# Graph attention on one core: warm-up matmuls, counts between merge steps, one layout for the bins, and a last block of 96 destinations

## The chip, the cores and the metric

The kernel runs on one core of a Trainium2 chip. The metric is the device time of one execution in microseconds (us), the median of several executions. A core has five engines with a queue each: TensorE (PE, matmuls, with its weight loads listed apart as PEld), VectorE (DVE), ScalarE (ACT), GpSimd (POOL) and SyncE (SP), which here only issues transfers. Engines wait for each other through semaphores.

## The reference, cut to what matters

```
num_nodes, in_features, out_features, num_edges, n_heads = 4096, 64, 64, 50000, 4
x_proj[h] = x @ weight[h]
score[h, i] = leaky( x_proj[h, src_i] . att_src[h] + x_proj[h, dst_i] . att_dst[h] )     # slope 0.2
output[h, dst_i] += exp(score[h, i]) * x_proj[h, src_i]                                  # all edges i
output[h, d] /= sum of exp(score[h, i]) over the edges i with dst_i = d, plus 1e-8
return output as [4096, 4 * 64]
```

Edges come as two lists of 50,000 node numbers, in no order. The work is a gather by source, a weight per edge and head, and a sum by destination.

## The kernel before, in words

**Keys.** Each of 128 partitions takes 391 edges. An edge becomes one number, `key`, which orders edges by group of source (16 groups of 256 nodes), then destination, then source within the group. VectorE computes it in two halves, L695 to L698, from the tiles `eS` and `eD`, which are loaded in two parts.

**First sort.** VectorE sorts the keys by compare-exchange steps on 128x512 tiles: `flip` (L190, L192) and `half` (L201, a pair of operations: minimum and maximum). `rows` sorts each partition, and `runs` then merges runs of eight partitions with the help of 32x32 transposes (`turn`, L230). Beside it ScalarE counts with 16 sign activations (`below`, L269) how many keys of each partition lie below each group bound, TensorE adds the counts of a run in two small matmuls (`counts`, L280), and it prepares the tables (`tables`, L404 to L425): `xa` with x and each source's part of the score, `adb` with each destination's part and an identity matrix. `store` (L261, SP) writes the sorted runs to DRAM. `bounds` (L289 to L295) turns the counts into the start and end of each stretch, `ws1` and `we1`. `fetch` converts the start to integer (`wi`, L352) and gathers `raw` from DRAM with two indirect transfers (L354, POOL): each partition gets the part of one run that belongs to its group.

**Second sort.** `group` merges again with VectorE, by destination now. ScalarE's 33 sign activations count against the bounds of 33 blocks of 125 destinations (BD), TensorE adds them, and VectorE turns them into offsets (`Stretches`, L310 to L320) between the last half steps. On these half steps also hang `relative` and `split` (L720 to L724), which prepare block 0 straight from the sorted keys. `turn` (80 matmuls, L372) and `warm` (5 matmuls, L377) use TensorE without anyone reading the result. The sorted keys `ki` are stored (L261), and five windows `win` are gathered from them (L354, POOL), one for every eight blocks.

**Bins.** `Windows.unpack(i)` (L442 to L447) splits a window into destination within the block and source, as bf16 tiles `tb`; VectorE does it for window 0, VectorE and POOL for the others. SP stores them in `gat_bins` in DRAM (L449). `load(b)` (L472, SP) reads a block's bins back, the same 8 KB into every partition (`bc`, four buffers). For blocks 0 and 1 `spread` does without DRAM: TensorE copies rows across partitions (L483) and ScalarE or VectorE writes them to `bc` (L485).

**The loop over 33 blocks.** `onehot(b)`: VectorE compares `bc` with the partition number, L498 for destinations and the lower 128 sources of a group, L501 for the upper 128. `gather(b, c)` in three chunks of 6, 6 and 4 tiles: TensorE multiplies the one-hots with `xa` and `adb` (L519, L521, L525), which gathers features and scores and forms the one-hot of destinations per edge; ScalarE writes exp of the scores (`ex`, L527) and the gathered rows (`xs`, L529). `weights` (L539) and `values` (L547): VectorE forms the edge weights `wv` and weighted features `val`. `sums`: TensorE adds them by destination into `acc` (L563 for the weights, L570 for the features). `take` (L624, L626): ScalarE copies `acc` to `aT`. `project` (L631), `invert` (L636), `give` (L644, with the store L646) multiply by `weight`, divide and write the output. The last block holds 4096 - 32 x 125 = 96 destinations; its features are summed into two tiles of their own, and its output is written in two halves.

All engine queues follow the order in which the code issues instructions, since the whole part runs under a manual schedule; nothing is reordered by a planner. The part under `tc.If` handles inputs whose stretches overflow a window, and doesn't run here.

Of the kernel before, what the change touches and what calls it, by code (L numbers as in the profile page):

```python
# [11 lines left out]
P = 128  # L12
# [26 lines left out]
def kernel(ctx: ExitStack, tc: tile.TileContext, x: bass.AP, edge_index: bass.AP,  # L39
# [22 lines left out]
    bin_dram = nc.dram_tensor("gat_bins", (8 * NI, 2, NR, W2), BF16).ap()  # L62
# [100 lines left out]
    Wbd = cst.tile([P, 2, P], F32)  # L163
    ws1 = cst.tile([P, 2], F32)
# [7 lines left out]
    class Sorter:  # L172
# [59 lines left out]
        def runs(self, to=None, fine=0, between=()):  # L232
# [12 lines left out]
            for m in range(1, 3):  # L245
                self.turn()
                self.opposed(m)
                for j in range(m - 1, -1, -1):
                    self.half(j)
                self.turn()  # L250
                last = fine if m == 2 else 0
                todo = list(between) if m == 2 else []
                for j in range(8, last - 1, -1):
                    self.half(j, to=to if m == 2 and j == last else None)
                    if todo:
                        todo.pop(0)(self.a[self.cur])
                assert not todo
# [26 lines left out]
    def bounds(pool, cps, nt, n, off, mask, nk, ws, we):  # L284

        ni = ws.shape[1] // len(cps)
        for i, ps in enumerate(cps):
            cnt = pool.tile([P, nt + 1], F32, name=f"cnt{i}")
            V.tensor_scalar(out=cnt[:], in0=ps[:], scalar1=-0.5, scalar2=RUN * n / 2, op0=OP.mult, op1=OP.add)  # L289
            for o, t in ((0, ws), (1, we)):  # L290
                pick = pool.tile([P, ni, nk], F32, name=f"pick{i}{o}")
                V.tensor_tensor(out=pick[:], in0=av(cnt[:], o, [nk, ni], [1, nk]),
                                in1=av(mask[:], 0, [0, ni], [1, nk]), op=OP.mult)
                V.tensor_reduce(out=t[:, i * ni:(i + 1) * ni], in_=pick[:], axis=AX, op=OP.add)
                V.tensor_tensor(out=t[:, i * ni:(i + 1) * ni], in0=t[:, i * ni:(i + 1) * ni],  # L295
                                in1=av(off[:], i, [0, ni]), op=OP.add)
# [60 lines left out]
    PAGE = 80  # L357

    def group(pool, pp, start, between=()):
# [8 lines left out]
        if between:  # L368

            turn = pp.tile([P, L], F32, name="turn")  # L370
            for i in range(PAGE):
                T.matmul(out=turn[:, 0:32], lhsT=identb[:], rhs=identb[:, 0:32], start=True, stop=True)  # L372
        st = Stretches(pool, counts(pool, pp, sgn, 8 * NI, [sel2[:]])[0])
        if between:
            warm = pp.tile([P, L], F32, name="warm")
            for i in range(5):
                T.matmul(out=warm[:], lhsT=identb[:], rhs=adb[:, 0:4, 0:P], start=True, stop=True)  # L377
# [53 lines left out]
    class Windows:  # L431
# [8 lines left out]
        def unpack(self, i, *engs):  # L440
# [7 lines left out]
            for k, eng in enumerate(engs):  # L448
                eng.dma_start(out=dataclasses.replace(bin_dram[8 * i, k], ap=[[2 * NR * W2, 8], [W2, NR], [1, W2]]),  # L449
                              in_=self.tb[:, i, k, :])  # L450
# [6 lines left out]
    class Blocks:  # L457
# [11 lines left out]
        def load(self, b):  # L469
            if b < ND:  # L470
                t = self.bcp.tile([P, 2, NT * W2], BF16, name="bc")
                nc.sync.dma_start(out=t[:], in_=dataclasses.replace(bin_dram[b], ap=[[0, P], [NT * W2, 2],  # L472
                                                                                    [1, NT * W2]]))
                self.bc[b] = t

        def spread(self, b, c, tb, row, copy):

            if c == 0:
                self.bc[b] = self.bcp.tile([P, 2, NT * W2], BF16, name="bc")
            t0, n = CH[c]  # L480
            ps = self.psx.tile([P, CH[0][1], PW], F32, name="ps")
            for i in range(n):
                T.matmul(out=ps[:, i, :], lhsT=av(identb[:], row(t0 + i), [0, P]), rhs=tb, start=(i % 2 == 0),  # L483
                         stop=True, skip_group_check=True)
            copy(out=av(self.bc[b][:], t0 * W2, [W2, n], [NT * W2, 2], [1, W2]),  # L485
                 in_=av(ps[:], 0, [PW, n], [W2, 2], [1, W2]))

        def onehot(self, b, t0=0, nt=NT, halves=(0, 1)):
            if b >= ND:
                return  # L490
            if t0 == 0 and halves[0] == 0:

                self.oh[b] = self.bp.tile([P, 3, NT * W2], BF16, name="oh")
            oh, bc = self.oh[b], self.bc[b]
            e = slice(t0 * W2, (t0 + nt) * W2)
            for i in halves:
                if i == 0:
                    V.tensor_scalar(out=oh[:, 0:2, e], in0=bc[:, :, e], scalar1=pF[:, 0:1], scalar2=None,  # L498
                                    op0=OP.is_equal)
                else:  # L500
                    V.tensor_scalar(out=oh[:, 2, e], in0=bc[:, 1, e], scalar1=pF[:, 1:2], scalar2=None,  # L501
                                    op0=OP.is_equal)

        def gather(self, b, c):
# [10 lines left out]
            ps = self.psx.tile([P, CH[0][1], PW], F32, name="ps")  # L515
            for i in range(n):
                t = t0 + i
                e = slice(t * W2, (t + 1) * W2)
                T.matmul(out=ps[:, i, P:P + XC], lhsT=oh[:, 1, e], rhs=xa[:, 2 * t, :], start=(i % 2 == 0), stop=False,  # L519
                         skip_group_check=True)  # L520
                T.matmul(out=ps[:, i, 0:S0], lhsT=oh[:, 0, e], rhs=adb[:, b, :], start=False, stop=False,  # L521
                         skip_group_check=True)
            for i in range(n):
                t = t0 + i
                T.matmul(out=ps[:, i, P:P + XC], lhsT=oh[:, 2, t * W2:(t + 1) * W2], rhs=xa[:, 2 * t + 1, :],  # L525
                         start=False, stop=True, skip_group_check=True)
# [25 lines left out]
        def sums(self, b, k):  # L552
# [3 lines left out]
            if k < 0:  # L556
                self.acc = self.psa.tile([P, AW], F32, name="acc")
                self.to = [self.acc[:, i * BD:(i + 1) * BD] for i in range(2)]
                if apart:
                    self.to = [self.psx.tile([P, CH[0][1], PW], F32, name="ps")[:, 0, 0:BD] for i in range(2)]  # L560
# [8 lines left out]
            for t in range(NT):  # L569
                T.matmul(out=self.to[k], lhsT=val[:, t, k * P:(k + 1) * P], rhs=xs[:, t, 0:BD],  # L570
# [38 lines left out]
    class Finish:  # L609
# [8 lines left out]
        def take(self, b, acc, at=0):  # L618
            n = acc.shape[-1]
            if n != BD:  # L620
# [4 lines left out]
            if n != BD:  # L625
                S.activation(out=self.aT[b][:, 2 * BD:AW], in_=acc[:, n - H:n], func=ACTF.Identity, bias=eps[:, 0:1])  # L626

        def project(self, b):
            self.pf = self.psf.tile([P, C], F32, name="pf")
            for k in range(2):  # L630
                T.matmul(out=self.pf[:, k * P:(k + 1) * P], lhsT=self.aT[b][:, k * BD:k * BD + P], rhs=Wbd[:, k, :],  # L631
# [6 lines left out]
        def give(self, b, parts=1):  # L638
# [3 lines left out]
            for k, eng in zip(range(parts), (nc.sync, nc.scalar)):  # L642
                h = slice(k * nh, (k + 1) * nh)
                V.tensor_tensor(out=res[0:BD, h], in0=av(self.pf[0:BD], k * nh * Dout, [Dout, nh], [1, Dout]),  # L644
                                in1=av(self.inv[0:BD], k * nh, [1, nh], [0, Dout]), op=OP.mult)
# [34 lines left out]
    with tc.tile_pool(name="sort1", bufs=1) as so1, tc.tile_pool(name="pre", bufs=1) as pr, \  # L680
# [3 lines left out]
        tF = so1.tile([P, EL], F32)  # L684
# [6 lines left out]
        for e, n in ((0, EH), (EH, EL - EH)):  # L691
# [3 lines left out]
            V.tensor_scalar(out=sli[:, c], in0=src, scalar1=SG - 1, scalar2=None, op0=OP.bitwise_and)  # L695
            V.tensor_scalar(out=tF[:, c], in0=sli[:, c], scalar1=1.0 - N, scalar2=None, op0=OP.mult)
            V.scalar_tensor_tensor(out=uF[:, c], in0=dst, scalar=float(SG), in1=tF[:, c], op0=OP.mult, op1=OP.add)
            V.scalar_tensor_tensor(out=key[:, c], in0=src, scalar=float(N), in1=uF[:, c], op0=OP.mult, op1=OP.add)  # L698
        tables(pr, pps, pp1)
        so.rows(1, EL)  # L700
        cps = counts(so1, pp1, sgn, NR, [sel1[:, 0, :], sel1[:, 1, :]])
        store(skey1, so.runs())
        bounds(so1, cps, NR, EL, off1, m16, NR, ws1, we1)
    with ExitStack() as st:
# [3 lines left out]
        class Lent:  # L708


            def tile(self, shape, dt, name):
                return blocks.sink.psf.tile(shape, dt, name=name, tag="pf")

# [15 lines left out]
        stretches = group(so2, Lent(), ws1[:], (relative, split))  # L729
# [8 lines left out]
        win.unpack(0, nc.sync, nc.sync)  # L738
# [15 lines left out]
        for i in range(1, NI):  # L754
            win.unpack(i, nc.sync, nc.sync)
        blocks.sums(0, 1)
        blocks.onehot(2)
# [65 lines left out]
```

## Time and profile before

| | |
|---|---|
| median of 5 executions | 292.8 us (292.29 to 293.94) |
| the profiled execution's own time | 290.6 us |
| its span, first to last instruction | 288.5 us |
| mean granted TensorE clock | 0.851 |
| busy: VectorE, TensorE, ScalarE, GpSimd | 261.4, 205.7, 190.8, 33.3 us |
| first sort stored (issue) | 68.20 us |
| second sort stored (issue) | 113.46 us |
| first whole one-hot of the loop, block 2 | 129.18 us |
| one block of the loop | 4.7 us |
| last output issued | 282.3 us |

In a row of the timeline the first number is the start in us from the span's start, the second the time until the group's last instruction ends, then engine, line, operation and operands as output<-input, and in brackets the idle time ahead of it with what ended it. `x2` means two instructions of a kind in a row. `SPq` is the issue of a transfer by SP, not the transfer itself. In the row PEclk each digit is TensorE's granted clock in tenths, in 40 equal slices of the span.

### The profile page before, as it was taken

To read this page: it belongs to the slowest core of one execution; us is meant where nothing else is said; L and a number is where in the kernel's file an instruction comes from. 1 tells how busy PE (TensorE), PEld (TensorE's weight loads), DVE (VectorE), ACT (ScalarE), POOL (GpSimd) and SP (SyncE) were. 2 spreads that over 40 slices of the span, in tenths; PEclk is the share of its full clock that TensorE was granted. 3 is DMA by queue.
4 is the path that set the end of the run, shared out by engine and by line. 5 is a ranking of instruction groups with operands and counts; after the bars stand their busy time and mean duration, and the time that the engine had idled before them with its cause. 6 is when DMAs were issued, how large, how long until landed. Compare 5 with 4: busy or idle time off the path is not lost.

```text
span 288.5 us, 8664 instructions
## 1 busy us (share of the span) xinstructions
PE 205.7 (71%) x3593; PEld 197.3 (68%) x3593; DVE 261.4 (91%) x528; ACT 190.8 (66%) x392; POOL 33.3 (12%) x81
## 2 busy tenths in 40 slices
PE   0000899992000008698999999999999999999980
PEld 0000599992000004498999999999999999999980
DVE  5999999997399999979999999999999999999960
ACT  2960620013399965757888888888888888888850
POOL 7882000000200000752000000000000000000000
PEclk9999975555555555869999999999999999999997
DMA  3007000001100001187868686868676777765011
GB/s 111 0 21 145 0 2 0 0 1 40 36 0 0 0 0 37 45 265 275 332 251 276 224 287 220 290 207 297 225 284 222 279 233 260 250 250 182 26 38 38
DMA packets 13328, 40.77 MB, mean 141 GB/s; under 512 B 3120, under 2 KB 8912, under 8 KB 9312
## 3 DMA queue, kind: packets, MB, share of 16 engines
q1 hardware_dynamic: 10768, 37.91, 37.5%
q10 hardware_dynamic: 1808, 1.56, 2.3%
q0 software_dynamic: 704, 0.66, 1.2%
q8 instruction: 30, 0.49, 0.7%
q14 instruction: 18, 0.15, 0.2%
HBM read 35.08 MB, written 5.05 MB: 139 GB/s over the span
## 4 chain that ended last, share of the span: by engine, by line


## 5 line engine op out<-in xcount | busy, mean ns | idle before, releaser
L529 ACT CAST xs<-ps 128x1200 bf16<-128x1200 f32 (+1 forms) x99 | 103.9, 1050 | 0.0
L547 DVE TENSOR_TENSOR val<-xs,wv 128x4096 bf16<-128x4096 bf16 (+1 forms) x34 | 75.4, 2219 | 0.4 <-ACT xs L529 0.2
L570 PE MATMUL acc<-xs,val 128*128 128x125 bf16 x1024 | 62.6, 220 | 0.0
L521 PE MATMUL ps<-adb,oh 128*128 128x136 bf16 x528 | 62.2, 225 | 0.0
L519 PE MATMUL ps<-xa,oh 128*128 128x72 bf16 x528 | 59.6, 197 | 2.1 <-ACT aT L624 1.1
L570 PEld LDWEIGHTS <-val 128*128 128x128 bf16 x1056 | 59.6, 99 | 0.2
L521 PEld LDWEIGHTS <-oh 128*128 128x128 bf16 x528 | 49.6, 99 | 1.3 <-issue 1.2
L519 PEld LDWEIGHTS <-oh 128*128 128x128 bf16 x528 | 47.4, 99 | 1.4 <-DVE oh L498 1.4
L498 DVE TENSOR_SCALAR oh<-bc,pF 128x4096 bf16<-128x4096 bf16 (+2 forms) x37 | 42.5, 1148 | 1.1 <-ACT bc L485 0.7
L527 ACT ACTIVATE ex<-ps 128x96 bf16<-128x96 f32 (+1 forms) x99 | 25.0, 252 | 23.2 <-PE ps L525 23.1
L201 DVE TENSOR_TENSOR sA<-sB 128x256 f32<-128x256 f32 (+2 forms) x104 | 37.2, 399 | 1.7
L201 DVE TENSOR_TENSOR sB<-sA 128x256 f32<-128x256 f32 (+2 forms) x98 | 35.1, 399 | 1.6
L525 PE MATMUL ps<-xa,oh 128*128 128x72 bf16 x528 | 33.5, 198 | 0.0
L280 PE MATMUL cnt_ps<-sgn,sel 128*128 128x17 f32 (+1 forms) x6 | 1.7, 390 | 39.1 <-ACT sgn L272 39.1
L280 PEld LDWEIGHTS cnt_ps<-sgn,sel 128*128 128x128 f32 x6 | 1.4, 317 | 39.2 <-issue 39.1
L525 PEld LDWEIGHTS <-oh 128*128 128x128 bf16 x528 | 26.5, 99 | 0.1
L421 PEld LDWEIGHTS at_ps<-uv,xT 64*128 64x128 f32 x130 | 26.3, 313 | 0.2 <-issue 0.2
L421 PE MATMUL at_ps<-uv,xT 64*128 64x4 f32 x130 | 26.4, 339 | 0.0
L501 DVE TENSOR_SCALAR oh<-bc,pF 128x2048 bf16<-128x2048 bf16 (+2 forms) x37 | 25.6, 692 | 0.0
L269 ACT ACTIVATE junk<-kr,nb 128x512 f32<-128x512 f32 x33 | 23.8, 722 | 1.1
L631 PE MATMUL pf<-Wbd,aT 128*128 128x128 f32 x132 | 22.6, 294 | 0.8 <-ACT aT L624 0.8
L404 PE MATMUL ps<-ident,wS 64*128 64x64 f32 x2 | 0.7, 352 | 28.2 <-DMA wS<-in_weight_dram 28.2
(144 smaller groups left out, 248.3 us busy)
## 6 DMA issues: line engine op xcount, KB each, us to landing
bc<-gat_bins SPq DMA_DIRECT2D x31, 1024.0 KB
out_dram<-res SPq DMA_DIRECT2D x32, 125.0 KB
eD<-in_edge_index_dram ACTq DMA_DIRECT2D x2, 195.0 KB
eS<-in_edge_index_dram SPq DMA_DIRECT2D x2, 195.0 KB
gat_bins<-tb SPq DMA_DIRECT2D x10, 32.0 KB
gat_sorted<-sA SPq DMA_DIRECT2D x1, 256.0 KB
gat_sorted<-ki SPq DMA_DIRECT2D x1, 256.0 KB
win<-gat_sorted,to POOLq DMA_INDIRECT x5, 2.6
```

What stands on the lines that cost most here:

```text
L201: V.tensor_tensor(out=av(d[:], o, [2 * h, n], [1, h]), in0=av(s[:], 0, [2 * h, n], [1, h]), in1=av(s[:], h, [2 * h, n], [1, h]), op=op)
L269: S.activation(out=junk[:], in_=v, func=ACTF.Sign, bias=nbnd[:, b:b + 1], scale=1.0, accum_out=sgn[:, b:b + 1])
L421: T.matmul(out=ps[:, b, :], lhsT=xT[:, b * step:b * step + P], rhs=uv[:, k, :], start=(b == 0), stop=True, skip_group_check=True)
L498: V.tensor_scalar(out=oh[:, 0:2, e], in0=bc[:, :, e], scalar1=pF[:, 0:1], scalar2=None, op0=OP.is_equal)
L501: V.tensor_scalar(out=oh[:, 2, e], in0=bc[:, 1, e], scalar1=pF[:, 1:2], scalar2=None, op0=OP.is_equal)
L519: T.matmul(out=ps[:, i, P:P + XC], lhsT=oh[:, 1, e], rhs=xa[:, 2 * t, :], start=(i % 2 == 0), stop=False, skip_group_check=True)
L521: T.matmul(out=ps[:, i, 0:S0], lhsT=oh[:, 0, e], rhs=adb[:, b, :], start=False, stop=False, skip_group_check=True)
L525: T.matmul(out=ps[:, i, P:P + XC], lhsT=oh[:, 2, t * W2:(t + 1) * W2], rhs=xa[:, 2 * t + 1, :], start=False, stop=True, skip_group_check=True)
L527: S.activation(out=av(ex[:], 2 * t0, [2, n], [2 * NT, 2 * H], [1, 2]), in_=av(ps[:], P, [PW, n], [1, 2 * H], [0, 2]), func=ACTF.Exp)
L529: S.copy(out=xs[:, t0:t0 + n, 0:P + XC], in_=ps[:, 0:n, 0:P + XC])
L547: V.tensor_tensor(out=av(val[:], h * Dout, [Dout, n], [C, NT], [1, Din]), in0=av(xs[:], S0, [0, n], [XW, NT], [1, Din]), in1=av(wv[:], h * ...
L570: T.matmul(out=self.to[k], lhsT=val[:, t, k * P:(k + 1) * P], rhs=xs[:, t, 0:BD], start=apart and t == 0, stop=(t == NT - 1), skip_group_c ...
```

## The change

1. Keys: three operations per half instead of four. The bits of the group are masked rather than those within the group, which saves the tile `tF`.
2. `bounds` returns its operations as a list of 15 steps, the conversion to integer (`wi1`) among them. `runs` takes a second list, `ahead`, and works one step off after each half step. Nine of them go into the first round of merges, six into the second. The count matmuls are issued ahead of `tables`.
3. `turn` and `warm` are gone. A function `busy(n)` issues n matmuls of 512 columns whose result nobody reads, into the buffer of `acc`: 9 behind the second sort's counts, 11 behind `longest` and ahead of window 0's use, 3 behind block 0's sums.
4. `gat_bins`, `bc` and the one-hots get another layout: the destinations and sources of a group of 128 edges lie side by side. A window's bins are stored by one transfer with runs of 512 B instead of two with runs of 256 B. L498 and `spread`'s copies become contiguous; L501 reads rows of 128 elements with gaps of 128.
5. In the last block the sums of features and the projection cover 96 destinations instead of 125 and 128.

```diff
-    bin_dram = nc.dram_tensor("gat_bins", (8 * NI, 2, NR, W2), BF16).ap()
+    bin_dram = nc.dram_tensor("gat_bins", (8 * NI, NR, 2, W2), BF16).ap()
...
-                todo = list(between) if m == 2 else []
+                todo = list(between if m == 2 else ahead)
...
+        steps.append(lambda: V.tensor_copy(out=wi[:], in_=ws[:]))
+        return [lambda keys, f=f: f() for f in steps]
...
         so.rows(9)
-        if between:
-
-            turn = pp.tile([P, L], F32, name="turn")
-            for i in range(PAGE):
-                T.matmul(out=turn[:, 0:32], lhsT=identb[:], rhs=identb[:, 0:32], start=True, stop=True)
         st = Stretches(pool, counts(pool, pp, sgn, 8 * NI, [sel2[:]])[0])
         if between:
-            warm = pp.tile([P, L], F32, name="warm")
-            for i in range(5):
-                T.matmul(out=warm[:], lhsT=identb[:], rhs=adb[:, 0:4, 0:P], start=True, stop=True)
+            busy(9)
...
-            for k, eng in enumerate(engs):
-                eng.dma_start(out=dataclasses.replace(bin_dram[8 * i, k], ap=[[2 * NR * W2, 8], [W2, NR], [1, W2]]),
-                              in_=self.tb[:, i, k, :])
+            nc.sync.dma_start(out=bin_dram[8 * i:8 * i + 8].rearrange("b g k e -> (b g) k e"), in_=tb)
...
-                    V.tensor_scalar(out=oh[:, 2, e], in0=bc[:, 1, e], scalar1=pF[:, 1:2], scalar2=None,
-                                    op0=OP.is_equal)
+                    V.tensor_scalar(out=av(oh[:], (2 * NT + t0) * W2, [W2, nt], [1, W2]),
+                                    in0=av(bc[:], (2 * t0 + 1) * W2, [2 * W2, nt], [1, W2]),
+                                    scalar1=pF[:, 1:2], scalar2=None, op0=OP.is_equal)
...
                 if apart:
-                    self.to = [self.psx.tile([P, CH[0][1], PW], F32, name="ps")[:, 0, 0:BD] for i in range(2)]
+                    self.n = N - b * BD
+                    self.to = [self.psx.tile([P, CH[0][1], PW], F32, name="ps")[:, 0, 0:self.n] for i in range(2)]
...
+            m = min(P, N - b * BD)
             for k in range(2):
-                T.matmul(out=self.pf[:, k * P:(k + 1) * P], lhsT=self.aT[b][:, k * BD:k * BD + P], rhs=Wbd[:, k, :],
+                T.matmul(out=self.pf[0:m, k * P:(k + 1) * P], lhsT=self.aT[b][:, k * BD:k * BD + m], rhs=Wbd[:, k, :],
...
-            V.tensor_scalar(out=sli[:, c], in0=src, scalar1=SG - 1, scalar2=None, op0=OP.bitwise_and)
-            V.tensor_scalar(out=tF[:, c], in0=sli[:, c], scalar1=1.0 - N, scalar2=None, op0=OP.mult)
-            V.scalar_tensor_tensor(out=uF[:, c], in0=dst, scalar=float(SG), in1=tF[:, c], op0=OP.mult, op1=OP.add)
-            V.scalar_tensor_tensor(out=key[:, c], in0=src, scalar=float(N), in1=uF[:, c], op0=OP.mult, op1=OP.add)
+            V.tensor_scalar(out=sli[:, c], in0=src, scalar1=2 * N - SG, scalar2=None, op0=OP.bitwise_and)
+            V.scalar_tensor_tensor(out=uF[:, c], in0=sli[:, c], scalar=float(N - 1), in1=src, op0=OP.mult, op1=OP.add)
+            V.scalar_tensor_tensor(out=key[:, c], in0=dst, scalar=float(SG), in1=uF[:, c], op0=OP.mult, op1=OP.add)
+        cps = counts(so1, pp1, sgn, NR, [sel1[:, 0, :], sel1[:, 1, :]])
         tables(pr, pps, pp1)
         so.rows(1, EL)
-        cps = counts(so1, pp1, sgn, NR, [sel1[:, 0, :], sel1[:, 1, :]])
-        store(skey1, so.runs())
-        bounds(so1, cps, NR, EL, off1, m16, NR, ws1, we1)
+        steps = bounds(so1, cps, NR, EL, off1, m16, NR, ws1, we1, wi1)
+        store(skey1, so.runs(ahead=steps[:9], between=steps[9:]))
...
+        def busy(n):
+
+            t = blocks.psa.tile([P, L], F32, name="warm", tag="acc")
+            for i in range(n):
+                T.matmul(out=t[:], lhsT=identb[:], rhs=adb[:, 0:4, 0:P], start=True, stop=True)
...
+        busy(11)
+        win.unpack(0)
...
         blocks.sums(0, 1)
+        busy(3)
```

## The prediction

> **What bounds the kernel now.** I read the page's slices first, then the timeline engine by engine, because the page's chain of waits is empty in this profile.
>
> ```profile
> DVE  5999999997399999979999999999999999999960
> PEclk9999975555555555869999999999999999999997
> ```
>
> A slice is 7.2 us. VectorE (DVE) is full but for the first and last slices, the tenth and eleventh (65 to 79 us, the end of the first sort) and the eighteenth (123 to 130 us, the start of the loop). TensorE's clock is at half from 39 to 114 us and again near 121 to 128 us. From 130 us on every engine is full: in the timeline each block of the loop takes 4.7 us (val at 136.10 and at 140.86), TensorE issues without a gap, and VectorE waits about 0.1 us per block for `ex`. Nothing in the change shortens that period. So the question is how much earlier the loop begins, which VectorE's first whole one-hot (L498, 129.18 us) marks, and what is saved after the last block.
>
> The first hole is where the sort is stored and fetched again:
>
> ```profile
> 68.20 0.34 SPq L261 DMA_DIRECT2D gat_sorted<-sA  x1
> ...
> 70.80 0.16 DVE L295 TENSOR_TENSOR we<-we,off 128x1 f32<-128x1 f32 x1
> 71.39 0.17 DVE L352 CAST wi<-ws 128x2 int32<-128x2 f32 x1 [0.44 <-issue]
> 72.39 1.06 POOL L354 DMA_INDIRECT raw<-gat_sorted,wi  x1 [48.98 <-DVE wi L352]
> ...
> 76.67 0.42 DVE L190 TENSOR_TENSOR sA<-raw 128x256 f32<-128x256 f32 x1 [5.11 <-DMA raw<-gat_sorted,wi]
> ```
>
> The gather waits for `wi`, the last of 15 small VectorE operations, all but the first of them behind the store's issue. The second sort has the same pair of transfers, with the offsets ready by 113.35 us:
>
> ```profile
> 113.46 0.32 SPq L261 DMA_DIRECT2D gat_sorted<-ki  x1
> ...
> 116.20 1.01 POOL L354 DMA_INDIRECT win<-gat_sorted,to  x1 [41.34 <-DVE oh L501]
> ```
>
> Here the store alone gates (the one-hot named was only the last to finish): 116.20 - 113.46 = 2.74 us from issue to gather. The start of the loop:
>
> ```profile
> 119.99 1.38 SPq L449 DMA_DIRECT2D gat_bins<-tb  x2
> 122.93 2.56 SPq L472 DMA_DIRECT2D bc<-gat_bins  x3
> ...
> 128.26 0.26 DVE L442 TENSOR_SCALAR t<-win 128x128 int32<-128x128 int32 x1 [1.17 <-DMA win<-gat_sorted,to]
> ...
> 129.18 1.40 DVE L498 TENSOR_SCALAR oh<-bc,pF 128x4096 bf16<-128x4096 bf16 x1 [0.42 <-DMA bc<-gat_bins]
> ```
>
> VectorE is not waiting for TensorE here but for two transfers: the last window, then block 2's bins.
>
> [...] cold, L377's five of 512 columns start 0.43 us apart here. [...]
>
> **Part 1, keys.** Each half loses one operation (L696, 0.31 us), so 0.62 us of VectorE. The second half has to wait for its `eS` load: ScalarE's first sign (L269), which needs all of `eS`, starts at 5.59 us. VectorE would now be there at 5.29, so 0.3 of the gain is lost. I take 0.3 us; bounds 0 and 0.62.
>
> **Part 2, counts and bounds.** The two count matmuls go ahead of the tables on TensorE: their inputs are done at 19.3 us, and TensorE is idle until 28.2. The 15 small operations go between half steps of the merges. The second sort shows what that costs:
>
> ```profile
> 107.51 0.76 DVE L201 TENSOR_TENSOR sA<-sB 128x256 f32<-128x256 f32 x2
> 108.19 0.19 DVE L310 TENSOR_SCALAR cnt<-cnt_ps 128x41 f32<-128x41 f32 x1
> 108.31 0.76 DVE L201 TENSOR_TENSOR sB<-sA 128x256 f32<-128x256 f32 x2
> ```
>
> Half steps are 0.80 us apart with or without one (99.67, 100.46, 101.25), so 15 cost 0 to 0.3 us; I take 0.1. The gather is then late for the store. By the second sort's 2.74 us it starts at 68.20 + 2.74 = 70.94, 1.45 us earlier. By the bytes it is less: half-microsecond windows show this store moving until 70.0 to 70.5, the second one until 115.0, 1.2 us ahead of its gather, which gives 71.7 at worst, 0.7 us earlier. I take 1.1, less 0.1: **1.0 us**, bounds 0.4 and 1.45. The whole second sort moves with it: ScalarE's 33 signs (done at 105.5, used at 108.2) start from the same `raw` and keep their slack.
>
> **Part 3, busy work and layout, up to the loop.** The 80 matmuls `turn` ran at 64 us, where nobody waited: removing them is worth nothing. busy(9) starts behind the second count at 106.4 instead of 108.44, as it no longer waits for VectorE's `cnt`: cold 9 x 0.43 = 3.8 us, done at 110.3, before its successor's input (110.64). So the clock can rise up to 2 us sooner, spread(0)'s first six matmuls take some 0.65 instead of 1.3 us, and VectorE's two waits for `bc` (0.30 and 0.39) shrink. That brings unpack(0) to at most 0.4 us earlier. busy(11) stands between the two transposes (ending 118.56) and spread(1) (120.11): warm 11 x 0.216 = 2.4 us, so spread(1) starts some 0.8 us late and wins it back at full clock; cold 4.7 us, 3.1 late. Behind it queue spread(1), ScalarE's `bc` copies, one-hot(1). VectorE has 1.17 + 0.42 = 1.6 us of waiting to absorb that. busy(3) waits for ScalarE's `aT` copies, and gather(2,0) is queued behind it; warm, its 0.65 us fall ahead of one-hot(2).
>
> The bins of a window are stored by one DMA instead of two. SP issues two in 1.38 us, so the last is out 0.69 us sooner and the loads start near 122.2. Thus block 2's bins would land near 128.5. VectorE's order has unpack(4) before one-hot(2), and its window comes from POOL's queue, not moved by this: 128.26 + 0.5 for the two unpack operations is 128.8, instead of 129.18. So 0.4 at most, though the loads now run into the last window's transfer sooner; with an earlier window as well 0.9. I take **0.3 us**, bounds -1.0 (cold busy(11), or a later window) and 0.9. The four later windows' stores (8 issues, 6.82 us on SP) become four; they lie beside the loop, and the load behind them (134.80) is needed three blocks later: nothing. The strided half of the one-hot (L501) keeps 128-element rows, 16, 6 or 4 of them[...]: I cost it at nothing, covered besides by about 0.1 us per block.
>
> **Part 4, last block.** Its 32 matmuls have 96 columns instead of 125[...]. The first 16 are hidden behind the second half of `val`; the other 16 save 0.19 us. The copies (0.26 each) and the projection's loads save hundredths. VectorE's `res` costs the same on fewer partitions. I take 0.2 us, bounds 0 and 0.35.
>
> **Sum.** 0.3 + 1.0 + 0.3 + 0.2 = 1.8 us off the profiled execution's 290.6 us (span 288.5 and 2.1 around it), so 288.8. The median of the runs, 292.8, is 2.2 above the profiled one; I carry the difference over: **291.0 us**. The ends together give -0.6 to 3.3 us, 289.5 to 293.4.
>
> **Rivals.** (a) The change does not do what it says: the clock is down at busy(11), and the first sort's gain is lost there. [...] Start 3.1 us late, 1.6 absorbed: 1.5 lost and the 0.3 not gained, 292.8. (b) [...] It decides from 0.16 us more per L501 on (1.8/31 + 0.1). [...] (c) All parts at their better end: store landed as early as in the second sort, keys 0.6, window earlier: 289.6.
>
> **How the numbers follow.** Forecast 0.65, (a) 0.19, (b) 0.04, (c) 0.12. A measurement tells apart 0.3%, 0.9 us. The forecast and (c) are faster, but 0.03 of the forecast stays within it; of (a), whose start may also be less late or later, 0.02 is faster, 0.14 within, 0.03 slower; (b) is slower. Faster 0.76, same 0.17, slower 0.07. The range 289.5 to 292.8 leaves out (b) and the slow half of (a), together about 0.14, and a little beyond (c).
>
> **What would show it.** After: the first gather (L362) 2.5 to 3.3 us behind its store and no small VectorE operations between; half steps still 0.80 apart; one-hot(2) 1.2 to 2 us earlier; clock full from about 111 us on; L495 (once L501) at 0.75 us; loop 4.7 us per block. A later one-hot(2), or L495 above 0.9, would make the prediction wrong.

## The result and the profile after

The median went from 292.51 to **291.43 us**, the two kernels being run side by side: ratio 0.9961, 95% interval 0.9947 to 0.9975, so 1.1 us faster, against 1.8 us forecast. A ratio is taken from the fast executions alone (a slow one is over 1.5% above the fastest of its kernel) and a median from all of them, so where many were slow, as 13 of 19 in e2 below, the two can point different ways. Executions of one kernel spread over some 4 us (before: 290.33 to 294.21), and the profiled execution of before, 290.6 us, was among the fastest of its kind. The profiled one of after took 291.15 us (span 289.4), near its own median. So the two spans, 288.5 and 289.4 us, don't show the gain; the stages have to be compared one by one.

VectorE's and the clock's rows of the page after:

```profile
DVE  5999999993599999858999999999999999999970
PEclk9999975555555559997999999999999999999997
```

The half clock now ends about a slice earlier (108 us, before 114). The hole at 65 to 79 us, two slices that read 7 and 3 before, reads 3 and 5: it comes sooner, and the small operations that partly filled it have moved into the sort. The hole at the start of the loop is wider (8, 5 and 8 where before had one 7). A part of the first sort and its hand-over, in the timeline after:

```profile
49.69 0.76 DVE L202 TENSOR_TENSOR sA<-sB 128x256 f32<-128x256 f32 x2
50.37 0.17 DVE L292 TENSOR_SCALAR cnt<-cnt_ps 128x17 f32<-128x17 f32 x1
50.49 0.76 DVE L202 TENSOR_TENSOR sB<-sA 128x256 f32<-128x256 f32 x2
...
67.86 0.34 SPq L262 DMA_DIRECT2D gat_sorted<-sA  x1
70.90 1.06 POOL L362 DMA_INDIRECT raw<-gat_sorted,wi  x1 [47.17 <-issue]
...
75.52 0.43 DVE L191 TENSOR_TENSOR sA<-raw 128x256 f32<-128x256 f32 x1 [7.68 <-DMA raw<-gat_sorted,wi]
```

The store is issued 0.34 us earlier (67.86; before 68.20), which is the keys. The gather follows it by 3.04 us instead of 4.19 and waits for the store alone, and VectorE resumes at 75.52 instead of 76.67. The small operations now between half steps cost nothing that can be read: with one or without, a half step of the first sort begins every 0.79 to 0.80 us. Then the start of the loop, where the forecast put the rest:

```profile
112.24 0.33 SPq L262 DMA_DIRECT2D gat_sorted<-ki  x1
114.98 0.94 POOL L362 DMA_INDIRECT win<-gat_sorted,to  x1 [41.61 <-DVE pick L323]
...
118.61 2.29 DVE L542 TENSOR_TENSOR val<-xs,wv 128x4096 bf16<-128x4096 bf16 x1
118.72 3.00 POOL L362 DMA_INDIRECT win<-gat_sorted,to  x1 [0.30 <-issue]
120.22 1.27 SPq L469 DMA_DIRECT2D bc<-gat_bins  x3
122.03 0.96 POOL L362 DMA_INDIRECT win<-gat_sorted,to  x1 [0.30 <-issue]
...
127.13 0.23 DVE L441 TENSOR_SCALAR t<-win 128x128 int32<-128x128 int32 x1 [1.45 <-DMA win<-gat_sorted,to]
...
129.10 0.23 DVE L441 TENSOR_SCALAR t<-win 128x128 int32<-128x128 int32 x1 [1.60 <-DMA win<-gat_sorted,to]
...
129.38 1.38 DVE L493 TENSOR_SCALAR oh<-bc,pF 128x4096 bf16<-128x4096 bf16 x1
```

The second sort is stored 1.22 us earlier (112.24; before 113.46), and the loads of bins start at 120.22 instead of 122.93, so block 2's bins no longer gate: the bracket on the last row is gone. Yet one-hot(2) starts at 129.38, in the profile of before at 129.18. Of the five gathers of windows the fourth took 3.00 us where the others took 0.94 to 0.96. It was issued 0.11 us after `val` of block 0 (L542) had begun, and ended 0.82 us after `val` ended. The fifth came behind it, and its rows reached VectorE at 129.10, behind the three loads of 1 MB.

Busy time by stretches of 4 us after, the third-last number of each row being TensorE's clock:

```profile
core 0: us, PE busy (x) PEld busy (x) DVE busy (x) ACT busy (x) POOL busy (x), PEclk, DMA share, GB/s
128.00:132.00 4.00, 1.93 (x23) 1.17 (x23) 2.80 (x6) 0.05 (x1) 2.58 (x3) 1.00 0.69 253
132.00:136.00 4.00, 4.00 (x61) 3.94 (x61) 3.33 (x3) 2.64 (x6) 0.00 (x0) 0.57 0.79 270
136.00:140.00 4.00, 4.00 (x91) 3.99 (x88) 3.88 (x6) 2.85 (x8) 0.00 (x0) 1.00 0.43 128
```

While VectorE waited for windows, TensorE had 1.93 us of work in 4, and in the next stretch the clock fell to 0.57. VectorE then waited 0.80 and 0.46 us for `ex` in the first two blocks of the loop: 1.26 us given back. From there on a block takes 4.71 us. The tail in the timeline, after:

```profile
278.66 2.36 DVE L542 TENSOR_TENSOR val<-xs,wv 128x2048 bf16<-128x2048 bf16 x2 [0.16 <-ACT xs L524]
...
282.76 0.48 DVE L642 TENSOR_TENSOR res<-pf,inv 96x128 f32<-96x128 f32 x2 [1.05 <-PE pf L629]
```

and before:

```profile
281.70 0.49 DVE L644 TENSOR_TENSOR res<-pf,inv 125x128 f32<-125x128 f32 x2 [1.52 <-PE pf L631]
```

The last `res` begins 4.10 us after the last `val` (278.66), before 4.57 (281.70 after 277.13); its wait for `pf` shrank from 1.52 to 1.05.

Read together for the two profiled executions: one-hot(2) 0.20 later, the loop's first blocks 1.26 longer, the tail 0.47 shorter, together 0.99; the last `res` is 1.06 later. So what was gained ahead of the second store had been lost before the loop's third block, compared with a lucky execution of before.

### The profile page after: what moved, and what is told of

It reads as the page before. It is cut to its first block, busy times and chain, and to the rows that moved or that the text cites. A ratio compares the mean times of both kernels' runs of the same rounds, so it can differ in the third digit from the quotient of the medians.

```text
span 289.4 us, 8530 instructions
## 1 busy us (share of the span) xinstructions
PE 204.8 (71%) x3531; PEld 194.7 (67%) x3531; DVE 259.1 (90%) x526; ACT 190.8 (66%) x392; POOL 34.2 (12%) x81
## 4 chain that ended last, share of the span: by engine, by line
## 5 line engine op out<-in xcount | busy, mean ns | idle before, releaser
L542 DVE TENSOR_TENSOR val<-xs,wv 128x4096 bf16<-128x4096 bf16 (+1 forms) x34 | 75.4, 2219 | 0.4 <-ACT xs L524 0.2
L567 PE MATMUL acc<-xs,val 128*128 128x125 bf16 x1024 | 61.8, 218 | 0.0
L567 PEld LDWEIGHTS <-val 128*128 128x128 bf16 x1056 | 58.6, 98 | 0.3 <-DVE val L542 0.3
L495 DVE TENSOR_SCALAR oh<-bc,pF 128x2048 bf16<-128x2048 bf16 (+2 forms) x37 | 25.6, 692 | 0.0
L629 PE MATMUL pf<-Wbd,aT 128*128 128x128 f32 (+1 forms) x132 | 23.1, 297 | 0.5 <-ACT aT L621 0.5
L560 PEld LDWEIGHTS <-xs 128*128 128x128 bf16 x528 | 18.7, 96 | 0.4
```

The lines of the kernel that those rows point to most:

```text
L495: V.tensor_scalar(out=av(oh[:], (2 * NT + t0) * W2, [W2, nt], [1, W2]), in0=av(bc[:], (2 * t0 + 1) * W2, [2 * W2, nt], [1, W2]), scalar1=p ...
L542: V.tensor_tensor(out=av(val[:], h * Dout, [Dout, n], [C, NT], [1, Din]), in0=av(xs[:], S0, [0, n], [XW, NT], [1, Din]), in1=av(wv[:], h * ...
```

## The experiments

**Theory W:** the 1.2 us won in the sorts reach the second store and the bins, but not the loop, because the last windows now decide: a gather is held on GpSimd by `val`, and its rows come behind the loads of bins. The rivals: the busy work holds TensorE's queue or fails to keep the clock; or one of the parts costs by itself. First each part alone on the kernel before. Each ratio is to executions of before in the same rounds, whose median was 291.82 us for e1 to e4, 292.49 for e5 to e8 and 292.00 for f1 to f4.

**e3, keys, counts and bounds alone.**

```diff
 (on before)
...
+        cps = counts(so1, pp1, sgn, NR, [sel1[:, 0, :], sel1[:, 1, :]])
         tables(pr, pps, pp1)
...
+        steps = bounds(so1, cps, NR, EL, off1, m16, NR, ws1, we1, wi1)
+        store(skey1, so.runs(ahead=steps[:9], between=steps[9:]))
```

> The kernel before with the keys in three operations and the bounds between merge steps, nothing else of the change. Prediction's sum: 0.3 + 1.0 = 1.3 us faster than before, 291.2; the traces of before and after show the second sort's store 1.22 us earlier. If the start of the loop absorbs part of it, between 291.2 and 292.2.

Measured 290.18 us, ratio 0.9947 (0.9928 to 0.9965), 1.55 us faster. In its timeline the second store is issued at 112.41, and the wait has moved to the last window:

```profile
119.65 2.29 DVE L555 TENSOR_TENSOR val<-xs,wv 128x4096 bf16<-128x4096 bf16 x1
120.22 2.55 POOL L362 DMA_INDIRECT win<-gat_sorted,to  x1 [0.31 <-issue]
...
129.00 0.23 DVE L450 TENSOR_SCALAR t<-win 128x128 int32<-128x128 int32 x1 [2.45 <-DMA win<-gat_sorted,to]
```

Parts 1 and 2 by themselves carry the whole gain of the change. So in the medians the 1.2 us do reach the end, and theory W is too strong as worded; what the late windows can have taken is what the earlier bins were to add. The held gather shows without any of the busy work: here it is the fifth, issued 0.57 us into `val` and ended 0.83 us after it.

**e4, layout and single store alone.**

```diff
 (on before)
-            for k, eng in enumerate(engs):
-                eng.dma_start(out=dataclasses.replace(bin_dram[8 * i, k], ap=[[2 * NR * W2, 8], [W2, NR], [1, W2]]),
-                              in_=self.tb[:, i, k, :])
+            nc.sync.dma_start(out=bin_dram[8 * i:8 * i + 8].rearrange("b g k e -> (b g) k e"), in_=tb)
...
```

> The kernel before with the new layout of bins and one-hots and one store for each window, nothing else of the change. Prediction: up to 0.4 us faster. Theory W: the bins' loads start about 1.2 us sooner and run ahead of the last window's gather, which lands no earlier or later, so 0 to 1 us slower: 292.5 to 293.5. The strided half of the one-hot stays at 0.75 us in both.

Measured 291.59 us, ratio 0.9994 (0.9963 to 1.0025): no difference to be seen. Its timeline at the fifth gather:

```profile
121.23 0.95 POOL L354 DMA_INDIRECT win<-gat_sorted,to  x1 [0.30 <-issue]
121.37 2.29 DVE L543 TENSOR_TENSOR val<-xs,wv 128x4096 bf16<-128x4096 bf16 x1
```

Here `val` came 0.14 us after the gather: the gather took its 0.95 us, VectorE waited for no window, and one-hot(2) began at 128.45. The two overlapped by 0.81 us all the same; what differs from after, where the gather took 3.00 us, is their order. VectorE then waited 0.49 us for `ex` and 0.39 for `xs`.

**e7, the busy work alone.**

```diff
 (on before)
-            turn = pp.tile([P, L], F32, name="turn")
...
-            warm = pp.tile([P, L], F32, name="warm")
...
+            busy(9)
...
+        busy(11)
...
+        busy(3)
```

> The kernel before with the busy matmuls (9, 11, 3) in the place of turn and warm, nothing else of the change. Theory W: within 0.6 us of before, 291.9 to 293.1. Theory C: most of the measured gain of 1.1 us, 291.4.

Measured 293.14 us, ratio 1.0018 (1.0002 to 1.0035): if anything slower. A row of its timeline:

```profile
129.73 0.23 DVE L434 TENSOR_SCALAR t<-win 128x128 int32<-128x128 int32 x1 [1.57 <-DMA win<-gat_sorted,to]
```

It has the same shape as after: the fourth gather took 2.83 us, VectorE waited 1.11 and 1.57 us for windows, and then 0.48 and 0.80 us for `ex`, with the clock at 0.77 in 132 to 134 us and at 0.50 in 134 to 136. The clock rises sooner as intended (1.00 from 110 us on, in before 0.50 up to 114), and `val` of block 0 comes at 119.50 instead of 120.20: now 0.28 us ahead of the fourth gather, in before 1.11 ahead of the fifth.

**e8, the last block alone.**

```diff
 (on before)
-                T.matmul(out=self.to[k], lhsT=val[:, t, k * P:(k + 1) * P], rhs=xs[:, t, 0:BD],
+                T.matmul(out=self.to[k], lhsT=val[:, t, k * P:(k + 1) * P], rhs=xs[:, t, 0:self.n],
...
```

> The kernel before with the last block's sums and projection on 96 destinations, nothing else of the change. Prediction: 0.2 us faster, 292.3; in the trace the last transfer issues 0.2 us closer behind the last values.

Measured 292.25 us, ratio 0.9988 (0.9961 to 1.0015): too small to tell from nothing. The last `res` begins 4.10 us after the last `val` (284.18 and 280.08), as in after, so 0.47 us are saved there. Up to the last block this is the code of before, and its timeline shows a less lucky execution of it:

```profile
130.47 0.23 DVE L442 TENSOR_SCALAR t<-win 128x128 int32<-128x128 int32 x1 [3.10 <-DMA win<-gat_sorted,to]
```

One-hot(2) began at 130.75, 1.57 us later than in the profile that the prediction was made from. The wait for the last window, 1.17 us there, was 3.10 here. Against this execution after is 1.37 us ahead at one-hot(2), about what the medians say.

The product of the four ratios is 0.9947 x 0.9994 x 1.0018 x 0.9988 = 0.9947; the change as a whole has 0.9961 (0.9947 to 0.9975). The parts roughly add up within these intervals, and no large interaction is needed.

**e2, the change without all 23 busy matmuls.**

```diff
 (on after)
-        if between:
-            busy(9)
...
-        busy(11)
...
-        busy(3)
```

> The changed kernel without any of the 23 busy matmuls. Theory W: TensorE is not what VectorE waits for before the loop, so within 0.6 us of the changed kernel, 290.8 to 292.0, with the clock down longer at the start of the blocks. Theory C: the busy matmuls carry the gain, so back to the kernel before or slower, 292.5 or more.

Measured 293.33 us, ratio to before 0.9978 (0.9946 to 1.001). The median lies in the range of theory C (292.5 or more), the ratio fits theory W, and its interval overlaps that of after: the time decides nothing. A part of its timeline (VectorE, SP):

```profile
120.63 0.41 DVE L346 TENSOR_REDUCE most<-mx_ps 1x2 int32<-1x256 f32 x1 [3.65 <-remote]
...
122.24 2.29 DVE L540 TENSOR_TENSOR val<-xs,wv 128x4096 bf16<-128x4096 bf16 x1
123.58 1.27 SPq L467 DMA_DIRECT2D bc<-gat_bins  x3
```

VectorE waited 3.65 us ahead of `most`, which reads `mx_ps`, the partitions' longest stretches turned by TensorE. TensorE, at half clock (0.50 up to 116 us, 0.55 in 116 to 118), had finished it by 118.07, so its clock explains at most 1.1 us of that wait; what ended the rest the trace does not name. `val` began only at 122.24, after the last gather's start (120.02): all five gathers took 0.94 to 1.06 us and VectorE waited for no window. But one-hot(2) began at 129.95. Against after, the loads came 3.4 us later and one-hot(2) 0.6. How much of this is the missing busy work is not shown: f3 below, which has busy(9) and busy(11), was profiled with the same wait and its loads at 123.62.

**e1, the change with windows 2 to 4 unpacked inside the loop**, each in the iteration that bears its number, so that one-hot(2) no longer stands behind them in VectorE's queue.

```diff
 (on after)
-        for i in range(1, NI):
-            win.unpack(i)
+        win.unpack(1)
...
-        blocks.run(1)
+        blocks.run(1, {i: (lambda i=i: win.unpack(i)) for i in range(2, NI)})
...
                     self.sink.give(b - 1)
+                if b in extra:
+                    extra[b]()
                 self.sums(b, 0)
...
```

> The changed kernel, with windows 2, 3 and 4 unpacked inside the loop (one each in the iterations of blocks 2, 3 and 4) instead of ahead of one-hot(2). Theory W (the last window gates the loop's start: after the change it lands at 129.1 us, while block 2's bins are there at 124.8): one-hot(2) starts near 125.5 instead of 129.4, busy(3) behind ScalarE's copies (128.1 to 128.9) then holds gather(2,0), so some 1 to 3 us less than the changed kernel, 288.4 to 290.4. Theory C (what holds the start is TensorE's clock and its queue): one-hot(2) is earlier but the first values are not, 291.4 as the changed kernel, within 0.4.

Measured 289.67 us, ratio to before 0.9921 (0.9896 to 0.9946), by the ratios 1.2 us better than the change. One-hot(2) began at 125.21, 4.17 us earlier than in after, which shows that there the windows had held it and the bins had not. Of the 4.17 us, 2.51 reach the last `res` (280.25); most of the rest was lost to the next wait (timeline, TensorE and VectorE):

```profile
125.21 1.27 DVE L493 TENSOR_SCALAR oh<-bc,pF 128x4096 bf16<-128x4096 bf16 x1
...
127.97 0.81 PE L717 MATMUL warm<-adb,identb 128*128 128x512 bf16 x3 [1.29 <-ACT aT L625]
...
132.72 0.23 DVE L534 TENSOR_TENSOR wv<-ex 128x128 bf16<-128x128 bf16 x1 [1.64 <-ACT ex L522]
```

busy(3) writes the buffer of `acc` and so waited for ScalarE's copies to `aT`; gather(2, 0), whose one-hot was ready by then, stood behind it until 128.62, and VectorE waited 1.64 us for its `ex`.

**e6, the same late unpacking on the kernel before.**

```diff
 (on before)
-        for i in range(1, NI):
-            win.unpack(i, nc.sync, nc.sync)
+        win.unpack(1, nc.sync, nc.sync)
...
```

> The kernel before with windows 2 to 4 unpacked inside the loop, nothing of the change. In its trace block 2's bins end VectorE's wait at 129.18 us, 0.4 us after the last window is unpacked, so here the bins would gate next: theory W gives only 0 to 0.5 us less than before, 292.0 to 292.5. If it gives as much as in the changed kernel (2 us or more), the single store has no part in it.

Measured 293.66 us, ratio 1.0025 (1.0002 to 1.0048): up to 0.5 us of gain was expected, and it is if anything slower. Its timeline:

```profile
129.65 1.29 DVE L498 TENSOR_SCALAR oh<-bc,pF 128x4096 bf16<-128x4096 bf16 x1 [3.11 <-DMA bc<-gat_bins]
```

In before the windows and the bins come at nearly the same time: with the windows out of the way the bins gate, and nothing is won. The late unpacking gained only on the kernel with the earlier bins.

**f1, loads 3 and 4 behind the last windows**, to take the 2 MB out of the way of the windows' rows.

```diff
 (on after)
-        for b in range(2, 5):
-            blocks.load(b)
+        blocks.load(2)
...
             win.unpack(i)
+        for b in (3, 4):
+            blocks.load(b)
```

> The changed kernel, but of the three loads of 1 MB ahead of the last windows' rows only block 2's is issued there; those of blocks 3 and 4 come after the store of the last window's bins. Theory W (the lead of 1.2 us is lost because the fourth gather is held on GpSimd by VectorE's val(0) and the rows of the last gather then lie behind 3 MB of loads): the hold stays (fourth gather near 3.0 us), but the fifth's rows land near 125 instead of 129, VectorE's two waits for win (1.45 and 1.60 us) shrink to under 0.5 together, one-hot(2) starts near 126.5 instead of 129.4; busy(3) then holds gather(2, 0) back, so a wait for ex of 0.5 to 1.5 us follows and the time is 289.8 (289.2 to 290.8). Theory H (the hold alone costs the lead, the loads nothing): windows no earlier, one-hot(2) at 129 or later, 291.4.

Measured 297.29 us, ratio to before 1.0183 (1.0153 to 1.0212): the time expected was far off, the start of it was not. Its timeline:

```profile
125.88 0.22 DVE L441 TENSOR_SCALAR t<-win 128x128 int32<-128x128 int32 x1
...
126.14 1.31 DVE L493 TENSOR_SCALAR oh<-bc,pF 128x4096 bf16<-128x4096 bf16 x1
...
128.40 4.83 SPq L447 DMA_DIRECT2D gat_bins<-tb  x4
...
128.61 2.65 POOL L446 TENSOR_SCALAR tb<-t,boff 128x128 bf16<-128x128 int32 x1
...
133.28 2.79 SPq L469 DMA_DIRECT2D bc<-gat_bins  x3
...
140.18 1.29 DVE L493 TENSOR_SCALAR oh<-bc,pF 128x4096 bf16<-128x4096 bf16 x1 [9.32 <-DMA bc<-gat_bins]
```

The fourth gather was held as before (2.82 us), the fifth ended at 122.98 as in after (122.99); but its rows were there when VectorE came to them at 125.88, no wait for `win` is left, and one-hot(2) began at 126.14 (expected 126.5). So the hold alone did not cost the lead; at least 3.2 us of the last window's delay (129.10 against 125.88 at most) came from standing behind the two loads that were moved. What I had not seen: on SP's queue the loads now stood behind four stores, each waiting for GpSimd's part of the unpacking (L445, L446), and GpSimd's operations were themselves slow beside VectorE's one-hot and `val` (up to 2.65 us, 0.60 undisturbed). Block 3's bins came 9.32 us late.

**f2, the same without busy(3).**

```diff
 (on f1)
-        busy(3)
```

> As the run before it, without busy(3) as well. Theory W: one-hot(2) near 126.5 and no wait for ex over 0.5 us after it, 288.5 (287.8 to 289.5): about 1.3 us less than with busy(3). Rival C (busy(3) is needed, the clock falls without it in the loop's first block): a wait for ex or xs of over 1 us in the first two blocks of the loop and no gain on the run before it, 289.8 or more.

Measured 298.74 us, ratio to before 1.0231 (1.02 to 1.0262). One-hot(2) at 126.22 as expected; then VectorE waited 7.53 us for block 3's bins, for the reason of f1, and only after that 1.38 us for `ex`. This run says nothing on busy(3).

**f3, the change without busy(3) alone.** The edit is that of f2, on after.

> The changed kernel without busy(3), all else as it was. Theory W: one-hot(2) still near 129.4, because the last window still lands near 129; with the transfers late, busy(3) at 128.1 is not in front of anything that VectorE waits for, so 291.4 (290.8 to 292.0), with the clock down near 131 to 135 in either case. Rival D (busy(3) alone is what spoils the change, the windows don't matter): 289.5 or less.

Measured 292.11 us, ratio to before 0.9985 (0.9961 to 1.0008): 0.1 us above the range of theory W, and no faster than after, so taking busy(3) away wins nothing by itself. Up to busy(3) this is the code of after, but the execution that was profiled (296.6 us, far above its median) took another course:

```profile
120.06 0.95 POOL L362 DMA_INDIRECT win<-gat_sorted,to  x1 [0.30 <-issue]
...
120.68 0.41 DVE L346 TENSOR_REDUCE most<-mx_ps 1x2 int32<-1x256 f32 x1 [3.65 <-remote]
...
122.29 2.29 DVE L542 TENSOR_TENSOR val<-xs,wv 128x4096 bf16<-128x4096 bf16 x1
123.62 1.27 SPq L469 DMA_DIRECT2D bc<-gat_bins  x3
...
129.17 1.31 DVE L493 TENSOR_SCALAR oh<-bc,pF 128x4096 bf16<-128x4096 bf16 x1
```

The clock stayed at half until past 117 us (0.50 up to 116, 0.65 in 116 to 118), although busy(9) ran from 104.69 us as in after (104.78), and VectorE had the wait of e2 ahead of `most`, with TensorE done by 117.90. `val` came behind all five gathers, none was held, no window was waited for, and one-hot(2) still began at 129.17. So the late windows held the loop in the execution of after that was profiled, but they are not the only thing that can put one-hot(2) near 129 us. And what busy(3) does while the windows are late, this trace cannot show.

**e5, late unpacking and no busy(3).** The edits of e1 and f2 together.

> The changed kernel with windows 2 to 4 unpacked inside the loop and without busy(3). Theory W: one-hot(2) near 125.5 us and nothing ahead of gather(2,0) on TensorE: 3 to 4 us less than the changed kernel, 287.5 to 288.5. Theory C: no less than 290.8.

Measured **287.63 us**, ratio to before 0.9853 (0.9821 to 0.9885). Timeline, VectorE:

```profile
125.24 1.28 DVE L493 TENSOR_SCALAR oh<-bc,pF 128x4096 bf16<-128x4096 bf16 x1
...
127.56 2.29 DVE L542 TENSOR_TENSOR val<-xs,wv 128x4096 bf16<-128x4096 bf16 x1 [0.21 <-ACT xs L524]
...
278.49 0.48 DVE L644 TENSOR_TENSOR res<-pf,inv 96x128 f32<-96x128 f32 x2 [1.05 <-PE pf L631]
```

One-hot(2) is 4.14 us earlier than in after and the last `res` 4.27 us earlier (278.49 and 282.76): the whole lead reaches the end. The wait of 1.64 us for `ex` is gone, and the fourth gather was still held (3.00 us), to no harm.

**f4, the same with 8 instead of 11 matmuls ahead of spread(1).**

```diff
 (on e5)
-        busy(11)
+        busy(8)
```

> The changed kernel with the unpacking of windows 2 to 4 put off into the loop, without busy(3), and with 8 in the place of the 11 idle multiplications ahead of spread(1). Theory W and the trace of the same with 11: the last of the 11 ended 0.6 us after the operands of spread(1) were there, and VectorE waited 0.64 us for bc; with 8 (0.65 us less of TensorE) this wait goes and the time is 287.1 (286.7 to 287.7) against 287.6. Rival A (the clock falls between the 8 and spread(1)): the wait for bc stays or grows, 287.6 to 288.3.

Measured 289.61 us, ratio to before 0.9907 (0.9878 to 0.9937), where 287.1 was expected. Timeline:

```profile
116.79 1.89 PE L717 MATMUL warm<-adb,identb 128*128 128x512 bf16 x8
...
121.50 0.62 DVE L493 TENSOR_SCALAR oh<-bc,pF 128x1536 bf16<-128x1536 bf16 x1 [0.61 <-ACT bc L481]
```

spread(1) began at 118.61 instead of 119.08, but ScalarE's copy of it began at 120.03, in e5 at 119.99: the wait of 0.64 us stayed at 0.61. It was not the busy matmuls that made it; what holds ScalarE there is open. The profiled execution took 287.5 us, that of e5 287.2. Its other executions reached 291.2, those of e5 289.3, and what sets them apart was not profiled. So the medians don't rank e5 and f4, nor do they say how much of e5's gain on e1 is busy(3). Both beat both kernels: the interval of f4 (up to 0.9937) lies below that of after (from 0.9947).

## Why the prediction was right, and where it was not

**Part 1, keys, 0.3 us: right.** The store came 0.34 us earlier. The wait for `eS` took its share as worked out: the second half's first operation waited 0.33 us for it.

**Part 2, counts and bounds, 1.0 us: right.** Parts 1 and 2 were to bring 1.3 us; the second store came 1.22 us earlier, and alone (e3) they gave 1.55 us (1.0 to 2.1 by the interval). The gather followed its store by 3.04 us, between the two values that the prediction had from the second sort (2.74) and, at worst, from the bytes (71.7 - 68.20 = 3.5).

**Part 3, up to the loop, a gain of 0.3 us: wrong in its step.** The forecast of the loads' start (122.2) was too late: with the lead of parts 1 and 2 and the earlier clock it was 120.22, and the bins stopped gating. The step that failed is "its window comes from POOL's queue, not moved by this: 128.26". The sorts' lead is counted apart in the prediction; taken off, that window should have come at 128.26 - 1.22 = 127.04, and it came at 129.10. The queue did start 1.22 us earlier, but then waited on VectorE's `val`, which the sorts and the earlier clock had brought 1.59 us earlier (118.61; before 120.20), and its rows came behind loads that had moved 2.7 us ahead. I had named "the loads now run into the last window's transfer sooner" and priced a later window only in the lower bound of -1.0; f1 puts it at 3.2 us or more. So one-hot(2) was not "1.2 to 2 us earlier" than in the profile of before but 0.20 later, which the prediction itself had named as a sign that it is wrong: the time held, the account of the loop's start did not. What part 3 was worth depends on the execution that it is held against: 1.22 + 0.20 + 1.26 = 2.7 us lost against the profiled one of before; against e8, which had 1.24 us of waits for `ex` in the loop's first blocks as well, 1.37 - 1.22 = 0.15 us won. The parts alone say 0.2 won by the layout (e4, far inside its interval, so not told from nothing) and 0.5 lost by the busy work (e7: 0.0018 x 292.5, its interval just clear of nothing).

The hold itself could have been read in the trace of before:

```profile
120.20 2.29 DVE L547 TENSOR_TENSOR val<-xs,wv 128x4096 bf16<-128x4096 bf16 x1
121.31 2.00 POOL L354 DMA_INDIRECT win<-gat_sorted,to  x1 [0.30 <-issue]
```

This fifth gather took 2.00 us where the others took 0.94 to 1.01, and ended 0.82 us after `val`. In after, issued 0.11 us behind `val`, the gather took 3.00 us; in e4, issued 0.14 us ahead of `val`, it took 0.95 us, and `val`, although second, still took its 2.29 us. Why `val` holds the gather, no run here shows.

**The clock.** In the profiled execution of after, busy(9) did what part 3 said, and more: full clock from 108 us (0.98 in 108 to 112, in before 0.50) instead of the 111 expected, and spread(0)'s first twelve matmuls in 1.47 us instead of 2.72. With busy(11) the clock was still 1.00, so rival (a), the clock down at busy(11), did not come about there; its 11 matmuls took 2.37 us up to the start of spread(1), 0.215 each as priced for full clock ("warm"), half of the 0.43 at which L377's start at half clock ("cold"). It is no sure thing: in the profiled execution of f3, the same code up to that point, the clock rose only past 117 us. In after the clock fell later, at 132 us (1.00 in 131 to 132, 0.52 in 132 to 133), behind the 4 us with 1.93 us of work for TensorE; in e5, with 3.78 to 4.00 us of work in each 4 us from 124 to 136 us, it stayed at 1.00. That the lack of work brought the fall is an estimate from these two and is not shown: in f3 TensorE had 1.75 us of work from 120 to 124 us, and the clock stayed at 1.00. The 1.26 us of waiting for `ex` that followed are a term that the sum lacked.

**Part 4, last block, 0.2 us: the gain was there, a little larger.** 0.47 us in the traces of after and e8, all of it in the wait for `pf` (1.52 to 1.05). The sum had 0.19 for TensorE's matmuls, and ScalarE's copy of the second tile did begin 0.19 sooner: 3.31 us after `val` (281.97), before 3.50 (280.63). The other 0.28 fell between the start of that copy and `res`, so in the copy (0.24 us, before 0.26) and the projection, which the sum put at hundredths. `res` cost the same on fewer partitions: 0.48 us for the two on 96, 0.49 on 125.

**Rival (b)**, a slower strided one-hot, is out, and the estimate that its gaps cost nothing held: L495 takes 0.74 to 0.75 us for 2048 elements in the loop (0.85 once, in its first block), L501 in before 0.75. One reading of the profile was loose: from 130 us on VectorE and TensorE are full in the page of before, but ScalarE is at eight tenths and GpSimd idle. **Rival (c)**, every part at its better end and an earlier window, failed at the window, which came later.

**The carry-over.** The sum was made against a profiled execution and moved by 2.2 us to the median, as if its stages were typical. They were not: in it VectorE waited 1.17 us for the last window and hardly for `ex`, in e8, the same code up to the last block, 3.10 and 1.24. The comparison of the two profiled executions gave +0.55 us (291.15 against 290.6), that of the medians -1.1 us. That the forecast of 291.0 came near 291.43 is in part luck: a loss that it did not see fell on waits that an execution of before like that of e8 has as well.

## What to carry to other kernels

When a transfer is brought forward, price what it now runs ahead of: the rows of the last of five small gathers came over 3 us later behind 3 MB of loads than behind 1 MB (129.10 us in after, 125.88 or sooner in f1), and that took what the earlier bins had won. Work that only one later stage needs should not stand in the same queue ahead of what the next stage needs: putting off three unpackings was worth nothing on the kernel before (ratio 1.0025) and at least as much again as the whole change on the kernel after (0.9921 against 0.9961, one-hot(2) at 125.21 instead of 129.38 us). And before a sum is made against one profiled execution, look how that execution stands among the others, and which of its waits could be the lucky one.

## What the runs showed of the hardware that I had not expected

- A window's indirect gather issued on GpSimd while VectorE ran `val` (two bf16 inputs, 4096 elements a partition, 2.29 us) ended 0.82 to 0.83 us after `val` in before, after, e3 and f1 alike; undisturbed it takes 0.95 us. Issued 0.14 us ahead of `val` it took 0.95 us, and `val` its 2.29 us (e4).
- GpSimd's own operations on 128 elements took longer too: L446 0.60 us undisturbed, 2.02 beside the whole one-hot (after) and 2.65 beside `val` (f1).
- Small VectorE operations between two dependent half steps of 512 columns cost nothing that can be read here: half steps stay 0.79 to 0.80 us apart with or without one.
